# Scores of a streaming encoder's attention as 64-row matmuls on the two halves of TensorE

## The chip, the cores and the metric

One core of a Trainium2 chip runs the kernel. The metric is the device time of one execution in microseconds (us), the median of the runs.

## The reference, cut to what matters

One layer of a hybrid encoder, for a prompt of 2048 frames and a sample of 32 frames that continues a running stream (256 past frames). Everything is float32.

```python
h = rmsnorm(x, norm_gain)
qa, ka, va, ga, qb, kb, vb, gb = split(h @ w_in)          # 8 x 512 columns
# A: 8 heads x 64; each 64-frame chunk reads itself and 8 chunks before, with a relative bias
scores_a = einsum('bcqhd,bckhd->bchqk', qc, kband) * 64 ** -0.5 + bias
oa = softmax(scores_a) @ vband
# B: 4 heads, each with two 64-wide q/k pairs (m) and one 128-wide value, causal over chunks
scores_b = einsum('bqhmd,bkhmd->bhmqk', rope(qb), rope(kb)) * 64 ** -0.5
p = softmax(where(mask, scores_b, -inf))
ob = subnorm((p[:, :, 0] - lam * p[:, :, 1]) @ vb)
y = rmsnorm(x + concat(oa * silu(ga), ob * silu(gb)) @ w_out, final_gain)
```

The outputs are y and the new k and v rows, for prompt and sample.

## The kernel before

The work goes in eight units `u` of 128 columns: four of A (two heads of 64 each) and four of B (one head with two q/k pairs of 64 each). In both cases a unit has two score problems with a contraction over 64, called `m` = 0 and 1 here and "heads" below. Each unit walks over 8 chunks of 256 frames (two tiles `tt` of 128). For one chunk, `chunk_qkv` projects q, k, v and the gate on TensorE (PE), transposes q and k, and puts them where the score matmuls read them. `attn_a` or `attn_b` then computes scores, softmax and the product with v. The output projection follows after all units, and the 32 frames of the sample are worked in between.

Full float32 precision is made of float32r matmuls: a value is split into a high part and a low part (value minus high), and a product is the sum of several passes. The projections (L254 to L256, L261 to L263) take three passes: high x high, high x low, low x high.

The scores take two passes before, with 128 rows for a contraction over 64. `ks[:, m]` holds, for head m, the high part of k in one half of the 128 rows and the low part in the other half. `qh[:, m]` holds the high part of q in both halves, `ql[:, m]` the low part in the half that meets k's high part, and zero in the other (L132, L133). So pass 1 (L378) gives q-high x (k-high + k-low), pass 2 (L379) q-low x k-high. The stacking takes two casts on ScalarE (L335, L336), four scaled copies on ScalarE (L339 to L342) and four VectorE subtractions (L337, L338, L343, L344) per chunk and unit; there are 64 such steps.

The score matmuls write a PSUM buffer of 512 columns (`s_psum`, three buffers, L102). In `attn_b`, for each block of up to 512 keys and each m: the two passes, a maximum on VectorE (L466), an exponential on ScalarE (L468). In `attn_a`, for each m and tt: the band of up to 640 keys in one or two pieces, with VectorE adding the bias and taking the maximum (L526).

The order of the work on each engine is not that of the text. A scheduler sets it when the kernel is built, from a simulated timeline, from priorities (`ahead(n)` shifts them) and from free buffers; PE then executes its list strictly as written. A list is shown here with one row for each matmul, `out<-in`, with the number of the buffer behind its name: `s_ps` are score buffers, `z_ps` projections, `o_ps` products with v, `t_ps` transposes.

Of the kernel before, what the change touches and what calls it, by code (L numbers as in the profile page):

```python
# [8 lines left out]
F32 = mybir.dt.float32  # L9
F32R = mybir.dt.float32r  # L10
AF = mybir.ActivationFunctionType
ALU = mybir.AluOpType
# [18 lines left out]
def hybrid_step(  # L31
# [54 lines left out]
    @contextmanager  # L86
    def ahead(n):
        tc.cur_priority -= n
        yield
        tc.cur_priority += n  # L90
# [7 lines left out]
    def st_tile(name, n, bufs=4):  # L98
        return pool.tile([P, n], F32, name=name, tag=name, bufs=bufs)

    def s_psum():
        return psum.tile([P, 512], F32, name="s_ps", tag="s", bufs=3)  # L102
# [23 lines left out]
    nlam = const.tile([P, 1], F32, name="nlam")  # L126
    hTs = const.tile([P, KT, 2 * NS], F32R, name="hTs")
    oTs = const.tile([P, KT, 2 * NS], F32R, name="oTs")
    qh = [const.tile([P, 2, 256], F32R, name=f"qh{i}") for i in range(2)]
    ql = [const.tile([P, 2, 256], F32R, name=f"ql{i}") for i in range(2)]  # L130
    for t in ql:
        POOL.memset(t[64:128, 0, :].bitcast(F32), 0.0)  # L132
        POOL.memset(t[0:64, 1, :].bitcast(F32), 0.0)  # L133
    qzs = const.tile([P, 2, NS], F32, name="qzs")
    POOL.memset(qzs, 0.0)

# [160 lines left out]
    def chunk_qkv(u, isB, c, hT, W, kss, vts):  # L297
        z = pool.tile([P, 2, 384], F32, name="z", tag="z", bufs=2)
        z0 = 0 if isB else 128
        for tt in range(2):  # L300
            zp = z_psum()
            project(hT, tt, W, zp[:, z0:384], slice(z0, 384))
            ACT.copy(out=z[:, tt, z0:384], in_=zp[:, z0:384])
        if not isB:
            qp = z_psum()
            project_T(hT, W, qp[:, 0:256], slice(0, 128))
        i = u % 4
        if isB:
            zr = z[:, :, 0:256].rearrange("p t (g e) -> p t g e", g=4)
            rope(zr, ropec[:, 2 * c:2 * c + 2, :], ropes[:, 2 * c:2 * c + 2, :], P, 2)  # L310
        for tt in range(2):
            t = 2 * c + tt
            if isB:
                SP.dma_start(out=bkpv[t * P:(t + 1) * P, i * P:(i + 1) * P], in_=z[:, tt, 128:256])
                SP.dma_start(out=bvpv[t * P:(t + 1) * P, i * P:(i + 1) * P], in_=z[:, tt, 256:384])
            elif t >= 12:
                r0 = (t - 12) * P
                SP.dma_start(out=akpv[r0:r0 + P, i * P:(i + 1) * P], in_=z[:, tt, 128:256])
                SP.dma_start(out=avpv[r0:r0 + P, i * P:(i + 1) * P], in_=z[:, tt, 256:384])
        with ahead(150):  # L320
            tp = t_psum()
            for tt in range(2):
                PE.transpose(out=tp[:, tt * P:(tt + 1) * P], in_=z[:, tt, 128:256], identity=ident)
                if isB:
                    PE.transpose(out=tp[:, 256 + tt * P:256 + (tt + 1) * P], in_=z[:, tt, 0:128], identity=ident)
            if c % 2 == 0:
                kss.append(pool.tile([P, 2, 512], F32R, name="ks", tag="ks", bufs=5))
            ks = kss[c // 2][:, :, (c % 2) * 256:(c % 2 + 1) * 256]
            tk = tp[:, 0:256]
            tq = tp[:, 256:512] if isB else qp[:, 0:256]  # L330
            par = parity[0]
            parity[0] ^= 1
            QH, QL = qh[par], ql[par]
            lo_, hi_ = slice(0, 64), slice(64, 128)
            ACT.copy(out=ks[lo_, 0, :], in_=tk[lo_])  # L335
            ACT.copy(out=ks[hi_, 1, :], in_=tk[hi_])  # L336
            DVE.tensor_tensor(ks[hi_, 0, :], tk[lo_], ks[lo_, 0, :].bitcast(F32), ALU.subtract)  # L337
            DVE.tensor_tensor(ks[lo_, 1, :], tk[hi_], ks[hi_, 1, :].bitcast(F32), ALU.subtract)  # L338
            ACT.activation(QH[lo_, 0, :], tq[lo_], AF.Copy, scale=0.125)  # L339
            ACT.activation(QH[hi_, 0, :], tq[lo_], AF.Copy, scale=0.125)  # L340
            ACT.activation(QH[lo_, 1, :], tq[hi_], AF.Copy, scale=0.125)
            ACT.activation(QH[hi_, 1, :], tq[hi_], AF.Copy, scale=0.125)  # L342
            DVE.scalar_tensor_tensor(QL[lo_, 0, :], tq[lo_], 0.125, QH[lo_, 0, :].bitcast(F32), ALU.mult, ALU.subtract)  # L343
            DVE.scalar_tensor_tensor(QL[hi_, 1, :], tq[hi_], 0.125, QH[hi_, 1, :].bitcast(F32), ALU.mult, ALU.subtract)  # L344
        yield QH, QL
        with ahead(-30):
            gp = z_psum()
            project_T(hT, W, gp[:, 0:256], slice(384, 512))
        if c % 2 == 0:
            vtt = pool.tile([P, 4, 2, P], F32R, name="vt", tag="vt", bufs=5)  # L350
            vts.append(vtt[:, 0:2])
            vts.append(vtt[:, 2:4])
        vt = vts[c]
        zv = z[:, :, 256:384]
        if isB:
            vh, vl = vt[:, :, 0, :], vt[:, :, 1, :]
            POOL.tensor_scalar(vh, zv, 1.0, 0.0, ALU.mult, ALU.add)
            POOL.tensor_tensor(vl, zv, vh.bitcast(F32), ALU.subtract)
        else:
            for m in range(2):  # L360
                src = zv[:, :, 64 * m:64 * m + 64]
                vh = vt[:, :, m, 64 * m:64 * m + 64]
                vl = vt[:, :, m, 64 - 64 * m:128 - 64 * m]
                POOL.tensor_scalar(vh, src, 1.0, 0.0, ALU.mult, ALU.add)
                DVE.tensor_tensor(vl, src, vh.bitcast(F32), ALU.subtract)
        gate = silu(gp[:, 0:256], P, 256)
        yield gate

    def qk(sp, QH, QL, ks, m, tt, k0, k1):
        if k1 - k0 == 1:  # L370
            if k0 % 2:
                k0 -= 1
            else:
                k1 += 1
        qs = slice(tt * P, (tt + 1) * P)
        w = (k1 - k0) * P
        kc = slice(k0 * P, k1 * P)
        PE.matmul(sp[:, 0:w], QH[:, m, qs], ks[:, m, kc], start=True, stop=False)  # L378
        PE.matmul(sp[:, 0:w], QL[:, m, qs], ks[:, m, kc], start=False, stop=True)  # L379
        return k0  # L380

    def split_p(blocks, kind):
# [64 lines left out]
    def attn_b(u, c, kss, vts, QH, QL):  # L447
# [3 lines left out]
        for tt in range(2):  # L451
# [6 lines left out]
            for b in range(nb):  # L458
                w = min(512, nk - b * 512)
                eb = []  # L460
                for m in range(2):
                    sp = s_psum()
                    qk(sp, QH, QL, kss[b], m, tt, 0, w // P)
                    if b == nb - 1:
                        DVE.memset(sp[0:64, w - 64:w], NEG)
                    DVE.tensor_reduce(nmx[:, m, b:b + 1], sp[:, 0:w], AX.X, ALU.max, negate=True)  # L466
                    e = e_tile("e")
                    ACT.activation(e[:, 0:w], sp[:, 0:w], AF.Exp, bias=nmx[:, m, b:b + 1], accum_out=sm[:, m, b:b + 1])  # L468
                    eb.append(e)
                es.append((eb, w))  # L470
# [35 lines left out]
    def attn_a(u, c, kss, vts, QH, QL, bias):  # L506
        c0 = max(0, c - 2)
        kss, vts = list(kss), list(vts)
        rows = {}
        for m in range(2):  # L510
            for tt in range(2):
                t = 2 * c + tt
                k0 = max(0, t - 4)
                w = (t - k0 + 1) * P
                with ahead(-250):
                    nmx = st_tile("nma", 1, 6)
                    e = pool.tile([P, BAND], F32, name="ea", tag="ea", bufs=4)
                    ev = e[:, 0:w]
                    mx = None
                    for j in range(k0 // 4, t // 4 + 1):  # L520
                        ka, kb = max(k0, 4 * j), min(t + 1, 4 * j + 4)
                        sp = s_psum()
                        kf = qk(sp, QH, QL, kss[j], m, tt, ka - 4 * j, kb - 4 * j)
                        wd, es, bs, ss = (kb - ka) * P, (ka - k0) * P, (ka - t + 4) * P, (ka - 4 * j - kf) * P
                        m2 = st_tile("mxa", 1, 8)
                        DVE.tensor_tensor_reduce(e[:, es:es + wd], sp[:, ss:ss + wd], bias[:, m, bs:bs + wd], 1.0,  # L526
                                                 NEG if mx is None else mx, ALU.add, ALU.max, m2)
                        mx = m2
                    DVE.tensor_scalar(nmx, mx, -1.0, 0.0, ALU.mult, ALU.add)  # L529
                    sm = st_tile("sma", 1, 6)  # L530
                    ACT.activation(ev, ev, AF.Exp, bias=nmx, accum_out=sm)  # L531
                    DVE.reciprocal(sm, sm)  # L532
                    POOL.tensor_scalar(ev, ev, sm[:, 0:1], 0.0, ALU.mult, ALU.add)  # L533
                rows[m, tt] = (e, k0)
        gate, vtc = yield
        vts = vts[:c] + [vtc]
        op = o_psum()
# [289 lines left out]
```

## Time and profile before

| what | before |
|---|---|
| median of 3 runs | 1624.31 us (1621.44 to 1624.65) |
| the profiled execution's time (its span) | 1624.3 us |
| PE busy | 1568.4 us, 97% |
| PE weight loads busy | 1453.1 us, 89% |
| VectorE (DVE) busy | 1110.5 us, 68% |
| ScalarE (ACT) busy | 997.0 us, 61% |
| GpSimd (POOL) busy | 654.6 us, 40% |

Busy time is the time in which an engine had an instruction under way. PE's matmuls overlap in its pipeline, so a matmul's own duration is longer than its share of the time; the distance from one start to the next is what it costs.

### The profile page before, as it was taken

How to read it: one execution, taken by the hardware profiler on the slowest of the kernel's cores; microseconds unless marked ns; L12 is line 12 of the kernel's file. 1: busy time of each engine (PE TensorE's matmuls, PEld its weight loads, DVE VectorE, ACT ScalarE, POOL GpSimd, SP SyncE). 2: the span in 40 equal slices, each digit the busy share in tenths (PEclk: the TensorE clock that was granted, in tenths of full speed). 3: DMA queues.
4: the chain of work that ended last, by engine and by line, in shares of the span. 5: the costliest groups of instructions: out<-in, count | busy, mean ns of one | idle time of the engine just before them, and what ended most of it. 6: DMA issues, size and time to landing. Idle time of an engine off the chain costs nothing.

```text
span 1624.3 us, 30799 instructions
## 1 busy us (share of the span) xinstructions
PE 1568.4 (97%) x10612; PEld 1453.1 (89%) x10612; DVE 1110.5 (68%) x3048; ACT 997.0 (61%) x2717; POOL 654.6 (40%) x1129
## 2 busy tenths in 40 slices
PE   7999999989999899999999999999999999989997
PEld 6899999978998799999998899999998999978885
DVE  5776757897588866675788856676789677743333
ACT  5776557777577766656777766565777666531111
POOL 5453434465145544353345544353446444520000
PEclk9999999999999999999999999999999999999999
DMA  7643453333332224335432153344423263334562
GB/s 275 225 172 119 176 208 131 131 122 130 125 137 86 97 102 178 122 128 195 162 136 79 66 186 124 131 148 167 159 89 129 84 240 131 131 132 161 172 210 67
DMA packets 92972, 233.92 MB, mean 144 GB/s; under 512 B 9776, under 2 KB 51888, under 8 KB 75376
## 3 DMA queue, kind: packets, MB, share of 16 engines
q1 hardware_dynamic: 92816, 231.96, 40.0%
q8 instruction: 84, 1.38, 0.3%
q14 instruction: 72, 0.59, 0.1%
HBM read 179.10 MB, written 53.74 MB: 143 GB/s over the span
## 4 chain that ended last, share of the span: by engine, by line
PE 77%; DVE 11%; ACT 5%; issue 3%; POOL 2%; DMA 1%; SPq 0%; DVEq 0%; POOLq 0%; ACTq 0%
PE z_ps L254 11%; PE z_ps L255 11%; PE z_ps L256 11%; PE t_ps L387 6%; PE z_ps L261 5%; PE z_ps L263 5%; PE z_ps L262 5%; PE s_ps L379 4%; PE s_ps L378 4%; DVE nmx L466 2%; PE o_ps L556 2%; PE o_ps L555 2%; DVE e L479 2%; DVE w L174 2%; PE o_ps L501 1%
## 5 line engine op out<-in xcount | busy, mean ns | idle before, releaser
L255 PE MATMUL z_ps<-w,hT 128*128 128x256 f32 (+2 forms) x1280 | 424.1, 332 | 4.1 <-POOL w L171 2.4
L254 PE MATMUL z_ps<-w,hT 128*128 128x256 f32 (+2 forms) x1280 | 424.7, 332 | 2.5 <-ACT hT L229 1.2
L256 PE MATMUL z_ps<-w,hT 128*128 128x256 f32 (+2 forms) x1280 | 424.1, 331 | 0.0
L255 PEld LDWEIGHTS z_ps<-w,hT 128*128 128x128 f32 x1280 | 243.5, 190 | 22.4 <-POOL w L171 3.4
L254 PEld LDWEIGHTS z_ps<-w,hT 128*128 128x128 f32 x1280 | 243.7, 190 | 19.3 <-ACT hT L229 1.7
L468 ACT ACTIVATE e<-s_ps,nmx 128x512 f32<-128x512 f32 (+3 forms) x320 | 199.1, 624 | 98.6 <-DVE nmx L466 90.5
L256 PEld LDWEIGHTS z_ps<-w,hT 128*128 128x128 f32 x1280 | 243.7, 190 | 14.1 <-issue 0.5
L397 DVE TENSOR_TENSOR pl<-t_ps,ph 128x512 fp32r<-128x512 f32 (+1 forms) x312 | 192.6, 623 | 77.8 <-ACT ph L396 75.4
L261 PE MATMUL z_ps<-hT,w 128*128 128x256 f32 x768 | 220.3, 287 | 1.7 <-DVE ql L344 1.7
L263 PE MATMUL z_ps<-hT,w 128*128 128x256 f32 x768 | 218.9, 285 | 0.0
L396 ACT CAST ph<-t_ps 128x512 fp32r<-128x512 f32 (+1 forms) x312 | 163.0, 535 | 90.5 <-PE o_ps L555 42.4
L262 PE MATMUL z_ps<-hT,w 128*128 128x256 f32 x768 | 218.4, 284 | 0.0
L378 PE MATMUL s_ps<-ks,qh 128*128 128x512 f32 (+2 forms) x544 | 194.0, 366 | 10.5 <-ACT e L468 7.8
L466 DVE TENSOR_REDUCE nmx<-s_ps 128x1 f32<-128x512 f32 (+3 forms) x320 | 187.9, 600 | 13.1 <-PE s_ps L379 9.8
L379 PE MATMUL s_ps<-ks,ql 128*128 128x512 f32 (+2 forms) x544 | 187.7, 357 | 0.1
L474 POOL TENSOR_SCALAR e<-e,da 128x512 f32<-128x512 f32 (+3 forms) x160 | 110.3, 704 | 168.5 <-DVE da L444 132.8
L261 PEld LDWEIGHTS z_ps<-hT,w 128*128 128x128 f32 x768 | 145.5, 190 | 4.9 <-PE o_ps L416 1.2
L262 PEld LDWEIGHTS z_ps<-hT,w 128*128 128x128 f32 x768 | 145.4, 189 | 2.1 <-issue 0.5
L263 PEld LDWEIGHTS z_ps<-hT,w 128*128 128x128 f32 x768 | 145.4, 189 | 1.6 <-issue 0.5
L533 POOL TENSOR_SCALAR ea<-ea,sma 128x640 f32<-128x640 f32 (+4 forms) x128 | 96.3, 754 | 115.3 <-DVE sma L532 98.7
L531 ACT ACTIVATE ea<-ea,nma 128x640 f32<-128x640 f32 (+4 forms) x128 | 97.3, 760 | 62.6 <-DVE nma L529 61.4
L378 PEld LDWEIGHTS s_ps<-ks,qh 128*128 128x128 f32 x544 | 102.2, 190 | 19.3 <-ACT e L468 12.0
(192 smaller groups left out, 3422.3 us busy)
## 6 DMA issues: line engine op xcount, KB each, us to landing
hT<-hTd SPq DMA_DIRECT2D x112, 1024.0 KB, 7.0
wraw<-in_w_in_dram SPq DMA_DIRECT2D x64, 256.0 KB, 5.0
hTd<-hT SPq DMA_DIRECT2D x8, 2048.0 KB, 7.3
oTd<-oT SPq DMA_DIRECT2D x64, 256.0 KB, 3.2
hT<-oTd SPq DMA_DIRECT2D x16, 1024.0 KB, 6.1
out_dram<-z SPq DMA_DIRECT2D x160, 64.0 KB, 1.6
xt<-in_x_prompt_dram SPq DMA_DIRECT2D x32, 256.0 KB, 5.4
y<-in_x_prompt_dram SPq DMA_DIRECT2D x32, 256.0 KB, 6.5
```

The lines of the kernel that those rows point to most:

```text
L254: PE.matmul(zp, hT[:, 0, k, ts], his[k][:, cols], start=(k == 0), stop=False)
L255: PE.matmul(zp, hT[:, 0, k, ts], los[k][:, cols], start=False, stop=False)
L256: PE.matmul(zp, hT[:, 1, k, ts], his[k][:, cols], start=False, stop=(k == KT - 1))
L261: PE.matmul(zp, his[k][:, cols], hT[:, 0, k, :], start=(k == 0), stop=False)
L262: PE.matmul(zp, his[k][:, cols], hT[:, 1, k, :], start=False, stop=False)
L263: PE.matmul(zp, los[k][:, cols], hT[:, 0, k, :], start=False, stop=(k == KT - 1))
L378: PE.matmul(sp[:, 0:w], QH[:, m, qs], ks[:, m, kc], start=True, stop=False)
L379: PE.matmul(sp[:, 0:w], QL[:, m, qs], ks[:, m, kc], start=False, stop=True)
L396: ACT.copy(out=hv, in_=tv)
L397: DVE.tensor_tensor(lv, tv, hv.bitcast(F32), ALU.subtract)
L466: DVE.tensor_reduce(nmx[:, m, b:b + 1], sp[:, 0:w], AX.X, ALU.max, negate=True)
L468: ACT.activation(e[:, 0:w], sp[:, 0:w], AF.Exp, bias=nmx[:, m, b:b + 1], accum_out=sm[:, m, b:b + 1])
```

## The change

The stacking goes. q and k stay as the transposes leave them: head 0 in rows 0 to 63, head 1 in rows 64 to 127. `ks[:, 0]` is the high part of both heads' k, `ks[:, 1]` the low part; `qh` and `ql` likewise lose the index m. That takes one ScalarE and one VectorE operation over 128 rows each for k, and the same for q. A score is now made by three matmuls of 64 rows: q-high x k-high, q-high x k-low, q-low x k-high. `qk` takes two score buffers and writes, for each of the three terms, first head 0's matmul and then head 1's. `attn_b` and `attn_a` ask for both buffers ahead of `qk`, and treat the two heads behind it; `attn_a`'s loop over m moves inside that over tt.

```diff
-            lo_, hi_ = slice(0, 64), slice(64, 128)
-            ACT.copy(out=ks[lo_, 0, :], in_=tk[lo_])
-            ACT.copy(out=ks[hi_, 1, :], in_=tk[hi_])
-            DVE.tensor_tensor(ks[hi_, 0, :], tk[lo_], ks[lo_, 0, :].bitcast(F32), ALU.subtract)
-            DVE.tensor_tensor(ks[lo_, 1, :], tk[hi_], ks[hi_, 1, :].bitcast(F32), ALU.subtract)
-            ACT.activation(QH[lo_, 0, :], tq[lo_], AF.Copy, scale=0.125)
...
-            DVE.scalar_tensor_tensor(QL[hi_, 1, :], tq[hi_], 0.125, QH[hi_, 1, :].bitcast(F32), ALU.mult, ALU.subtract)
+            ACT.copy(out=ks[:, 0, :], in_=tk)
+            DVE.tensor_tensor(ks[:, 1, :], tk, ks[:, 0, :].bitcast(F32), ALU.subtract)
+            ACT.activation(QH, tq, AF.Copy, scale=0.125)
+            DVE.scalar_tensor_tensor(QL, tq, 0.125, QH.bitcast(F32), ALU.mult, ALU.subtract)
...
-        PE.matmul(sp[:, 0:w], QH[:, m, qs], ks[:, m, kc], start=True, stop=False)
-        PE.matmul(sp[:, 0:w], QL[:, m, qs], ks[:, m, kc], start=False, stop=True)
+        terms = ((QH, 0), (QH, 1), (QL, 0))
+        for n, (q, part) in enumerate(terms):
+            for m in range(2):
+                hs = slice(64 * m, 64 * m + 64)
+                PE.matmul(sps[m][:, 0:w], q[hs, qs], ks[hs, part, kc], start=(n == 0), stop=(n == 2))
...
-                for m in range(2):
-                    sp = s_psum()
-                    qk(sp, QH, QL, kss[b], m, tt, 0, w // P)
+                sps = [s_psum() for _ in range(2)]
+                qk(sps, QH, QL, kss[b], tt, 0, w // P)
+                for m, sp in enumerate(sps):
...
+                for j in range(k0 // 4, t // 4 + 1):
+                    ka, kb = max(k0, 4 * j), min(t + 1, 4 * j + 4)
+                    sps = [s_psum() for _ in range(2)]
+                    kf = qk(sps, QH, QL, kss[j], tt, ka - 4 * j, kb - 4 * j)
```

PE's list moves with it. The first place is where `attn_b` begins on a chunk in the second unit of B; the score buffers are 7007 (head 0), 7013 (head 1) and 7019 (head 0 of the next block) before, and L416 closes the chunk ahead. Before:

```order
L416 MATMUL o_ps_6848<-sq_6910,onesd_72 128x256
L378 MATMUL s_ps_7007<-ks_5604,qh1_85 128x512
L378 MATMUL s_ps_7013<-ks_5604,qh1_85 128x512
L378 MATMUL s_ps_7019<-ks_6150,qh1_85 128x512
L379 MATMUL s_ps_7007<-ks_5604,ql1_87 128x512
L379 MATMUL s_ps_7019<-ks_6150,ql1_87 128x512
L379 MATMUL s_ps_7013<-ks_5604,ql1_87 128x512
```

The same place in PE's list of the changed kernel; the score line is L372 there, 7043 and 7044 are the two heads of the first block, and 7057 is head 0 of the next.

```order
L372 MATMUL s_ps_7043<-ks_5640,qh1_85 128x512
L372 MATMUL s_ps_7044<-ks_5640,qh1_85 128x512
L409 MATMUL o_ps_6890<-sq_6952,onesd_72 128x256
L372 MATMUL s_ps_7043<-ks_5640,qh1_85 128x512
L372 MATMUL s_ps_7044<-ks_5640,qh1_85 128x512
L372 MATMUL s_ps_7043<-ks_5640,ql1_87 128x512
L372 MATMUL s_ps_7044<-ks_5640,ql1_87 128x512
L372 MATMUL s_ps_7057<-ks_6182,qh1_85 128x512 x2
L372 MATMUL s_ps_7057<-ks_6182,ql1_87 128x512
```

Here the two heads of the first block alternate, but for a 128-row matmul between them; the third buffer goes to head 0 of the next block, whose head 1 (7058) stands further down.

The second place is on PE some 80 rows later in the same chunk, where all three buffers are in use. Before, each head's two passes stand between other work:

```order
L378 MATMUL s_ps_7067<-ks_5604,qh1_85 128x512
L379 MATMUL s_ps_7067<-ks_5604,ql1_87 128x512
L254 MATMUL z_ps_7691<-w_5198,hT_7331 128x384
L255 MATMUL z_ps_7691<-w_5198,hT_7331 128x384
L256 MATMUL z_ps_7691<-w_5198,hT_7331 128x384
```

In the changed kernel, 7123 and 7124 are the two heads of one block there:

```order
L372 MATMUL s_ps_7123<-ks_6182,qh1_85 128x512 x2
L372 MATMUL s_ps_7123<-ks_6182,ql1_87 128x512
L380 MATMUL t_ps_7272<-ident_67,e_6765 128x128
L380 MATMUL t_ps_7272<-ident_67,e_6831 128x128 x2
L495 MATMUL o_ps_7209<-pl_7241,vt_6315 128x256
L493 MATMUL o_ps_7209<-ph_7240,vt_6315 128x256
L494 MATMUL o_ps_7209<-ph_7240,vt_6315 128x256
L372 MATMUL s_ps_7124<-ks_6182,qh1_85 128x512 x2
L372 MATMUL s_ps_7124<-ks_6182,ql1_87 128x512
```

The three passes of head 0 stand together, six 128-row matmuls follow, and then come the three passes of head 1.

## Rows read from the trace of the kernel before

**Rows 1.** The page's head: span, and busy time of each engine (share, instructions).
```profile
span 1624.3 us, 30799 instructions
...
PE 1568.4 (97%) x10612; PEld 1453.1 (89%) x10612; DVE 1110.5 (68%) x3048; ACT 997.0 (61%) x2717; POOL 654.6 (40%) x1129
```

**Rows 2.** Busy us by stretch: length, engines (instructions), clock, DMA share, GB/s.
```profile
600.00:800.00 200.00, 199.29 (x1470) 190.61 (x1469) 133.25 (x419) 126.03 (x339) 81.96 (x171) 1.00 0.41 148
```

**Rows 3.** Waits of PE: waiter, releaser, us in total, times, longest.
```profile
PE t_ps L226 <- POOL xt L209: 11.6, 2, 9.9
PE s_ps L378 <- ACT e L468: 7.8, 12, 1.2
...
PE s_ps L378 <- ACT qh L340: 1.6, 2, 1.4
```

**Rows 4.** Timeline of PE, six score matmuls: start us, modelled us, instruction.
```profile
995.32 0.39 PE L378 MATMUL s_ps<-ks,qh 128*128 128x512 f32 x1
995.55 0.39 PE L379 MATMUL s_ps<-ks,ql 128*128 128x512 f32 x1
995.78 0.28 PE L378 MATMUL s_ps<-ks,qh 128*128 128x256 f32 x1
995.90 0.28 PE L379 MATMUL s_ps<-ks,ql 128*128 128x256 f32 x1
996.02 0.34 PE L378 MATMUL s_ps<-ks,qh 128*128 128x384 f32 x1
996.19 0.34 PE L379 MATMUL s_ps<-ks,ql 128*128 128x384 f32 x1
996.37 0.28 PE L262 MATMUL z_ps<-hT,w 128*128 128x256 f32 x1
```

**Rows 5.** Groups by shape, the score's first pass: count | busy, mean ns | idle before.
```profile
L378 PE MATMUL s_ps<-ks,qh 128*128 128x512 f32 x280 | 114.1, 411 | 6.6 <-ACT e L468 4.8 <-ACT qh L340 1.6 <-ACT qh L342 0.2
...
L378 PE MATMUL s_ps<-ks,qh 128*128 128x256 f32 x176 | 51.0, 297 | 3.4 <-ACT e L468 3.0 <-ACT qh L342 0.4
...
L378 PE MATMUL s_ps<-ks,qh 128*128 128x384 f32 x88 | 31.4, 360 | 0.5 <-DVE mxa L526 0.5
```

**Rows 6.** Timeline of PE where 32-row transposes (32*128) stand among 128-row work.
```profile
604.84 0.38 PE L592 MATMUL t_ps<-ident,kvs 128*128 128x128 f32 x2
605.15 0.24 PE L593 MATMUL t_ps<-ident,zs 32*128 32x32 f32 x1
605.24 0.22 PE L594 MATMUL t_ps<-ident,zs 32*128 32x32 f32 x1
605.30 0.22 PE L595 MATMUL t_ps<-ident,gate 32*128 32x32 f32 x1
605.45 0.39 PE L502 MATMUL o_ps<-pl,vt 128*128 128x256 f32 x1
605.68 0.28 PE L500 MATMUL o_ps<-ph,vt 128*128 128x256 f32 x1
605.80 0.28 PE L501 MATMUL o_ps<-ph,vt 128*128 128x256 f32 x1
```

**Rows 7.** Timeline of PE at a second such place.
```profile
765.81 0.27 PE L325 MATMUL t_ps<-ident,z 128*128 128x128 f32 x1
766.01 0.43 PE L633 MATMUL t_ps<-ident,es 32*128 32x32 f32 x5
766.37 0.39 PE L261 MATMUL z_ps<-hT,w 128*128 128x256 f32 x1
766.60 0.28 PE L262 MATMUL z_ps<-hT,w 128*128 128x256 f32 x1
```

**Rows 8.** Groups by shape on ScalarE: count | busy, mean ns | idle before.
```profile
L287 ACT ACTIVATE gabs<-gate 128x256 f32<-128x256 f32 x64 | 26.7, 417 | 15.6 <-DVE gate L286 14.8
...
L335 ACT CAST ks<-t_ps 64x256 fp32r<-64x256 f32 x64 | 23.1, 361 | 20.6 <-PE t_ps L325 11.8 <-PE t_ps L323 8.1
...
L339 ACT ACTIVATE qh<-t_ps 64x256 fp32r<-64x256 f32 x32 | 12.0, 376 | 14.2 <-DVE ks L338 13.8
```

More of the change, by code (lines that the diff above doesn't have):

```diff
@@ L128, in hybrid_step @@
     oTs = const.tile([P, KT, 2 * NS], F32R, name="oTs")
[L129 to L133, printed above, removed]
+    qh = [const.tile([P, 256], F32R, name=f"qh{i}") for i in range(2)]
+    ql = [const.tile([P, 256], F32R, name=f"ql{i}") for i in range(2)]
     qzs = const.tile([P, 2, NS], F32, name="qzs")
@@ L333, in chunk_qkv @@
             QH, QL = qh[par], ql[par]
-            lo_, hi_ = slice(0, 64), slice(64, 128)
-            ACT.copy(out=ks[lo_, 0, :], in_=tk[lo_])
-            ACT.copy(out=ks[hi_, 1, :], in_=tk[hi_])
-            DVE.tensor_tensor(ks[hi_, 0, :], tk[lo_], ks[lo_, 0, :].bitcast(F32), ALU.subtract)
-            DVE.tensor_tensor(ks[lo_, 1, :], tk[hi_], ks[hi_, 1, :].bitcast(F32), ALU.subtract)
-            ACT.activation(QH[lo_, 0, :], tq[lo_], AF.Copy, scale=0.125)
[L340 to L343, printed above, removed]
-            DVE.scalar_tensor_tensor(QL[hi_, 1, :], tq[hi_], 0.125, QH[hi_, 1, :].bitcast(F32), ALU.mult, ALU.subtract)
+            ACT.copy(out=ks[:, 0, :], in_=tk)
+            DVE.tensor_tensor(ks[:, 1, :], tk, ks[:, 0, :].bitcast(F32), ALU.subtract)
+            ACT.activation(QH, tq, AF.Copy, scale=0.125)
+            DVE.scalar_tensor_tensor(QL, tq, 0.125, QH.bitcast(F32), ALU.mult, ALU.subtract)
         yield QH, QL
@@ L367, in chunk_qkv, with qk @@
         yield gate
-    def qk(sp, QH, QL, ks, m, tt, k0, k1):
+    def qk(sps, QH, QL, ks, tt, k0, k1):
         if k1 - k0 == 1:
@@ L509, in attn_a @@
         rows = {}
[L510 to L515, printed above, removed]
-                    nmx = st_tile("nma", 1, 6)
[L517 to L529, printed above, removed]
+        for tt in range(2):
+            t = 2 * c + tt
+            k0 = max(0, t - 4)
+            w = (t - k0 + 1) * P
+            with ahead(-250):
+                es_ = [pool.tile([P, BAND], F32, name="ea", tag="ea", bufs=4) for _ in range(2)]
+                mxs = [None, None]
+                for j in range(k0 // 4, t // 4 + 1):
+                    ka, kb = max(k0, 4 * j), min(t + 1, 4 * j + 4)
+                    sps = [s_psum() for _ in range(2)]
+                    kf = qk(sps, QH, QL, kss[j], tt, ka - 4 * j, kb - 4 * j)
+                    wd, es, bs, ss = (kb - ka) * P, (ka - k0) * P, (ka - t + 4) * P, (ka - 4 * j - kf) * P
+                    for m in range(2):
+                        m2 = st_tile("mxa", 1, 8)
+                        DVE.tensor_tensor_reduce(es_[m][:, es:es + wd], sps[m][:, ss:ss + wd], bias[:, m, bs:bs + wd], 1.0,
+                                                 NEG if mxs[m] is None else mxs[m], ALU.add, ALU.max, m2)
+                        mxs[m] = m2
+                for m in range(2):
+                    ev = es_[m][:, 0:w]
+                    nmx = st_tile("nma", 1, 6)
+                    DVE.tensor_scalar(nmx, mxs[m], -1.0, 0.0, ALU.mult, ALU.add)
@@ L533, in attn_a @@
                     POOL.tensor_scalar(ev, ev, sm[:, 0:1], 0.0, ALU.mult, ALU.add)
-                rows[m, tt] = (e, k0)
+                    rows[m, tt] = (es_[m], k0)
         gate, vtc = yield
```

## The prediction

> **What bounds the kernel now.** I read the busy totals first: TensorE (PE) is busy 1568.4 of 1624.3 us, so at most 55.9 us of the span are not matmul [rows 1]. The table by stretches shows that this is no average over unlike stages: in a stretch of 200 us in the middle PE is busy 199.3 us, with VectorE at 133 and ScalarE at 126 [rows 2]. The list of PE's waits says the same from the other side: the longest is the start, 11.6 us for the first normalised x; the waits of the score matmuls for a free score buffer come to 7.8 us, and those for the stacked q to 1.6 us [rows 3]. So the time is the sum of what PE's instructions take one after another, in the order in which the scheduler has written them. A change is priced by what it does to that sum; what it saves on ScalarE and VectorE counts only where PE waited for it.
>
> What a matmul costs is the distance between starts, since the durations shown are those of a pipeline. The timeline of PE has six score matmuls in a row [rows 4]: 995.32 to 995.55 to 995.78 is 0.23 us for 512 columns, 995.78 to 995.90 to 996.02 is 0.12 for 256, 996.02 to 996.19 to 996.37 is 0.175 for 384. Cost goes by columns alone, about 0.45 ns each.
>
> **The change part by part.**
>
> *Three passes instead of two.* There are 280 first passes of 512 columns, 176 of 256 and 88 of 384 [rows 5], and as many second passes. Now: 560 x 0.23 + 352 x 0.12 + 176 x 0.175 = 128.8 + 42.2 + 30.8 = 201.8 us. With three passes 840 x 0.23 + 528 x 0.12 + 264 x 0.175 = 302.7 us. A matmul of 64 rows streams as many columns as one of 128, so without any overlap the change costs +100.9 us.
>
> *Overlap of the two halves.* If the halves of the array work side by side, a matmul that stands directly behind one of the other head is free. How often it does is in PE's order, which is fixed before the run, and the kernel's own text (head 0, head 1, head 0, ...) is not what the scheduler made of it. Of the 1632 score matmuls only few keep an other-head neighbour, as the second of the two places shown with the change tells: with three score buffers, only one is usually free, so one head's three passes go out alone, other work follows, and the other head's three come later. Counted along the whole order, 353 neighbours are of different heads and 807 of the same; paired off, 94 matmuls of 512, 36 of 384 and 84 of 256 columns can be hidden: 94 x 0.23 + 36 x 0.175 + 84 x 0.12 = 38.0 us. No row here shows two halves at once (the 32-row matmuls of this trace all use the same rows), so the bounds are 0 and 38.0. I take 38.0, since different halves share neither weights nor a score buffer.
>
> The Trainium skill, page "TensorE: Matmul & The Clock Gate", section "Part 3: Packing small matmuls — row/col tiling", says that matmuls on distinct row groups start about 4 ns apart and that matmuls never overtake one another. By it the 38.0 us are gained, and not more, since a head's partner that stands behind other work cannot be pulled forward; by the rows alone it could be anything from 0.
>
> *Changing the height of the array.* Before, the prompt's matmuls are nearly all 128 rows high. Now the score matmuls stand in 472 runs among 128-row matmuls (308 of them three long), and every run is entered and left. What that costs is shown by the sample's few 32-row transposes [rows 6]. From the second 128-row transpose (two begin at 604.84 and take 0.11 each, so it starts at 604.95) it is 0.20 us to the first 32-row one, 0.09 over its 0.11. The first 32-row step is 0.09 where the next is 0.06: +0.03. The step out is 0.15: +0.09. The first 128-row matmul behind takes 605.45 to 605.68 = 0.23 where the next take 0.12: +0.11. In all 0.32 us. A second place [rows 7]: from 765.81 to 766.60 is 0.79 us for one transpose (0.11), five 32-row ones (5 x 0.06) and one matmul of 256 columns (0.12), 0.53 together: 0.26 us. That a 64-row run pays the same is not shown. From below it could be nothing, from above 0.32; the nearest rows say 0.26 to 0.32, and I take 0.30: 472 x 0.30 = 141.6 us.
>
> *Weight loads.* Each added matmul brings a load. In rows 4 the loads don't show in the distance between starts. In 32-row mode a transposition with its load has a step of 0.06 us (605.24 to 605.30) [rows 6], of which 32 columns at 0.45 ns are 0.014; so between 0 and 0.046 us of a load can stand open. I take 0, the reading of rows 4, and keep 1632 x 0.046 = 75 us for the range.
>
> *Stacking.* Two 64-row casts of k at 0.36 us and four 64-row scalings of q at 0.38 [rows 8] become one of each over 128 rows, at about 0.42 by the 128x256 activation [rows 8]; four VectorE operations become two. Over 64 steps that is 64 x (2.24 - 0.84) = 90 us of ScalarE, hidden under PE's work almost entirely: PE waited 1.6 us for it [rows 3]. The four memsets of ql at the start run beside the 11.6 us wait for x. With PE later by a tenth and the other engines lighter, some of the 55.9 us of idle PE time goes; the start stays, so at most 44 us. On the other hand both buffers of a pair are now filled before the second is emptied, which could double the 7.8 us wait for buffers. Between -44 and +8 I take -10.
>
> *Sum.* The profiled execution's span, 1624.3 us, is the median of the runs shown, 1624.31. 1624.3 + 100.9 - 38.0 + 141.6 - 10 = 1818.8; I say 1820.
>
> **The rivals.**
>
> No overlap of the halves: everything else as above, without the 38.0: 1857 us. For it: nothing in the trace shows two matmuls at once. Against: separate rows, buffers and weights.
>
> Open weight loads: in half-height mode the load of a head's next pass waits for the pass in front, as 807 neighbours of the same head invite. 1857 plus up to 75, 1857 to 1932 us. Against: the loads are covered in rows 4, and the 32-row steps of 0.06 us leave little. The Trainium skill, same page and section, says that a weight load overlaps a running matmul only where the row groups differ; rows 4 disagree at full height, and no row has half height.
>
> Cheap change of height: 128 to 64 rows costs little although 128 to 32 doesn't. With 0 to 0.15 us a run it is 1624.3 + 100.9 - 38.0 - 10 = 1677 to 1748 us: still slower, because of the order.
>
> Half-height matmuls at half price: PE keeps the two halves as separate queues, so that each 64-row matmul costs half, wherever its partner stands. The scores then take 151 us, 50 less than now. This alone gives 1574 us and is faster than before from the point where a run's two changes cost less than 50 / 472 = 0.11 us; at 0.30 it would be 1574 + 142 = 1716. Against it: matmuls start in the order written in every stretch that I read, and rows 6 and 7 show 0.26 to 0.32. With a price close to 0.11 it would end as no change.
>
> **How the numbers follow.** Forecast with the pairs overlapping and switches at 0.26 to 0.32: 40%, with its own range 1795 to 1840. No overlap: 20%. Open loads: 15%. Cheap change of height: 18%. Half price: 7%, of which 4 end faster, 1 the same, 2 slower still. For 8 in 10 I leave out the top of the open loads and the lower half of the cheap changes: 1700 to 1890 us. A measurement of this kernel tells about 0.2% (3 us) from no change; beyond that faster 4%, the same 1%, slower 95%.
>
> **What the profile after would show.** PE's matmul count grows by 544 and its busy share stays near 97%. The score line has 1632 matmuls of 64 rows. Runs of one head step by 0.23 us at 512 columns; a pair of different heads starts almost together, then steps by 0.23. Into and out of a run of three PE's timeline shows about 0.1 us of extra distance at each of several places, 0.3 in all, and over an undisturbed stretch the same projection work takes longer by that. ScalarE's busy time falls by about 90 us. PE's waits for other engines don't grow. Wrong would be: starts at the edges of a run no farther apart than inside (then 1680 to 1720); distances of 0.28 us or more between the passes of one head at 512 columns (then towards 1900); or a new long wait of PE for a score buffer, which the sum has at 8 us at most.

## The result and the profile after

The changed kernel takes 1816.75 us (median of 4 runs, 1815.9 to 1819.11), the kernel before 1624.32; the ratio is 1.1187, with a 95% interval of 1.1171 to 1.1203. It is slower by 192 us.

The page of the changed kernel, its head and the score line (the columns are those of [rows 1] and [rows 5]):

```profile
span 1814.1 us, 31318 instructions
...
PE 1779.2 (98%) x11156; PEld 1490.7 (82%) x11156; DVE 1055.9 (58%) x2920; ACT 911.5 (50%) x2461; POOL 659.0 (36%) x1125
...
L372 PE MATMUL s_ps<-ks,qh 64*128 64x512 f32 (+2 forms) x1088 | 297.3, 398 | 0.6 <-ACT e L461 0.6
...
L372 PE MATMUL s_ps<-ks,ql 64*128 64x512 f32 (+2 forms) x544 | 169.0, 354 | 0.0
```

Against [rows 1], PE has 544 matmuls more and is idle for 34.9 us instead of 55.9; ScalarE is 85 us less busy, VectorE 55. Most of that relief lies beside a PE that has become longer; what of it PE got back is told further down.

PE's waits after, answering to [rows 3]:

```profile
PE t_ps L223 <- POOL xt L206: 11.0, 2, 10.8
...
PE s_ps L372 <- ACT e L461: 0.6, 1, 0.6
```

The waits of the score matmuls for a buffer fell from 7.8 us to 0.6, and the one for the stacked q is gone. The time is in PE's own list. Its timeline at the second place that was shown with the change, with the first of the two score runs:

```profile
564.54 0.28 PE L494 MATMUL o_ps<-ph,vt 128*128 128x256 f32 x1
564.66 0.39 PE L266 MATMUL z_ps<-w,hTs 128*64 128x512 f32 x1
564.98 0.72 PE L372 MATMUL s_ps<-ks,qh 64*128 64x512 f32 x2
565.55 0.39 PE L372 MATMUL s_ps<-ks,ql 64*128 64x512 f32 x1
565.87 0.55 PE L380 MATMUL t_ps<-ident,e 128*128 128x128 f32 x3
```

At [rows 4] a matmul of 512 columns had 0.23 us to the next start. Here L266 has 0.32 (564.66 to 564.98), the two passes with q-high together 0.57 instead of 0.46, and the last pass 0.32 instead of 0.23. So 0.09 us are lost going into the run, about 0.10 on its second matmul and 0.09 going out. The weight loads (PEld) of the same place:

```profile
564.55 0.14 PEld L266 LDWEIGHTS z_ps<-w,hTs 128*64 128x64 f32 x1
564.98 0.29 PEld L372 LDWEIGHTS s_ps<-ks,qh 64*128 64x128 f32 x2 [0.30 <-issue]
565.32 0.18 PEld L372 LDWEIGHTS s_ps<-ks,ql 64*128 64x128 f32 x1
```

The load of the run's third matmul starts at 565.32, a whole step ahead of that matmul at 565.55. The load of its first matmul does not start ahead: it starts at 564.98 together with the matmul. Over the trace, a load in full-height work starts 0.003 us behind the start of the matmul in front of its own; at a change of height the first load starts with its own matmul (0.002 us ahead), and the second one starts 0.107 us behind that matmul's start (medians). The second matmul is late by nearly the same 0.10 us. That the late loads are what delays the matmuls is a reading of these rows; no run tests it.

The next place shows the fourth piece, and what a pair does: both heads side by side, six 64-row matmuls in a row.

```profile
980.39 0.28 PE L493 MATMUL o_ps<-ph,vt 128*128 128x256 f32 x1
980.51 0.28 PE L494 MATMUL o_ps<-ph,vt 128*128 128x256 f32 x1
980.72 0.74 PE L372 MATMUL s_ps<-ks,qh 64*128 64x512 f32 x4
981.29 0.40 PE L372 MATMUL s_ps<-ks,ql 64*128 64x512 f32 x2
981.62 0.39 PE L495 MATMUL o_ps<-pl,vt 128*128 128x256 f32 x1
981.84 0.28 PE L493 MATMUL o_ps<-ph,vt 128*128 128x256 f32 x1
981.96 0.28 PE L494 MATMUL o_ps<-ph,vt 128*128 128x256 f32 x1
```

Six matmuls of 512 columns take 980.72 to 981.62 = 0.90 us, not 6 x 0.23 = 1.38: the halves do overlap. But 980.51 to 980.72 is 0.21 where 256 columns take 0.12, and behind the run 981.62 to 981.84 is 0.22 before the step is 0.12 again. A run thus pays 0.09 + 0.10 + 0.09 + 0.10. Over the whole trace the medians of these four, each the distance to the next start less the usual one for the same columns, are 0.092, 0.104, 0.088 and 0.104 us, 0.39 together.

### The profile page after: what moved, and what is told of

Its sections match the earlier page's. It is cut to its first block, busy times and chain, and to the rows that moved or that the text cites. A ratio compares the mean times of both kernels' runs of the same rounds, so it can differ in the third digit from the quotient of the medians.

```text
span 1814.1 us, 31318 instructions
## 1 busy us (share of the span) xinstructions
PE 1779.2 (98%) x11156; PEld 1490.7 (82%) x11156; DVE 1055.9 (58%) x2920; ACT 911.5 (50%) x2461; POOL 659.0 (36%) x1125
## 4 chain that ended last, share of the span: by engine, by line
PE 93%; DVE 2%; DMA 2%; issue 1%; ACT 1%; POOL 0%; SPq 0%; DVEq 0%; POOLq 0%; ACTq 0%
PE s_ps L372 18%; PE z_ps L251 12%; PE z_ps L252 12%; PE z_ps L253 11%; PE t_ps L380 7%; PE z_ps L258 5%; PE z_ps L259 5%; PE z_ps L260 5%; PE o_ps L549 2%; PE o_ps L550 2%; PE o_ps L493 2%; PE o_ps L495 2%; PE o_ps L494 2%; PE z_ps L265 1%; PE z_ps L266 1%
## 5 line engine op out<-in xcount | busy, mean ns | idle before, releaser
L372 PE MATMUL s_ps<-ks,qh 64*128 64x512 f32 (+2 forms) x1088 | 297.3, 398 | 0.6 <-ACT e L461 0.6
L258 PE MATMUL z_ps<-hT,w 128*128 128x256 f32 x768 | 224.6, 292 | 0.0
L259 PE MATMUL z_ps<-hT,w 128*128 128x256 f32 x768 | 222.1, 289 | 0.0
L260 PE MATMUL z_ps<-hT,w 128*128 128x256 f32 x768 | 221.6, 289 | 0.0
L372 PEld LDWEIGHTS s_ps<-ks,qh 64*128 64x128 f32 x1088 | 141.4, 185 | 78.9 <-issue 29.0
L372 PE MATMUL s_ps<-ks,ql 64*128 64x512 f32 (+2 forms) x544 | 169.0, 354 | 0.0
```

The source lines that it names most:

```text
L258: PE.matmul(zp, his[k][:, cols], hT[:, 0, k, :], start=(k == 0), stop=False)
L259: PE.matmul(zp, his[k][:, cols], hT[:, 1, k, :], start=False, stop=False)
L260: PE.matmul(zp, los[k][:, cols], hT[:, 0, k, :], start=False, stop=(k == KT - 1))
L372: PE.matmul(sps[m][:, 0:w], q[hs, qs], ks[hs, part, kc], start=(n == 0), stop=(n == 2))
```

## The experiments

**e1: the change of height alone.** The half of `ql` that the kernel before multiplies by zero can be left out without changing the result, so its second pass can have 64 rows while everything else stays.

```diff
-        PE.matmul(sp[:, 0:w], QL[:, m, qs], ks[:, m, kc], start=False, stop=True)
+        hs = slice(64 * m, 64 * m + 64)
+        PE.matmul(sp[:, 0:w], QL[hs, m, qs], ks[hs, m, kc], start=False, stop=True)
```

> The kernel before, with its second pass alone (q-low x k-high) on 64 rows; the half left out of it is zero anyway, so columns, passes and stacking stay as they are. PE's order has 514 runs of 64-row matmuls, 492 of them a single one. Theory A (from the changed kernel's trace: 0.09 us into a run, 0.10 on the second matmul in it, 0.09 out of it, 0.10 on the second matmul behind it): a run of one pays 0.09 + 0.09 + 0.10 = 0.28 us, 514 x 0.28 = 146 us, less up to 35 us of waits for score buffers that go when PE is later: 1735 to 1770 us. Theory B (changing the height is cheap; the changed kernel is slow by its third pass and by slow 64-row matmuls): 1625 to 1660 us.

Measured: 1775.32 us, ratio 1.0927 (1.0902 to 1.0952), +150 us for work that is otherwise the same: in the traces, 10610 of PE's 10612 matmuls stand at the same place in the order as before. Theory B falls; theory A is low by 5 to 40 us. A run of one in this kernel's timeline:

```profile
586.54 0.28 PE L502 MATMUL o_ps<-ph,vt 128*128 128x256 f32 x1
586.66 0.40 PE L378 MATMUL s_ps<-ks,qh 128*128 128x512 f32 x1
586.99 0.49 PE L380 MATMUL s_ps<-ks,ql 64*128 64x512 f32 x1
587.41 0.39 PE L254 MATMUL z_ps<-w,hT 128*128 128x256 f32 x1
587.63 0.28 PE L255 MATMUL z_ps<-w,hT 128*128 128x256 f32 x1
587.75 0.28 PE L256 MATMUL z_ps<-w,hT 128*128 128x256 f32 x1
```

L378 has 0.33 us (+0.10), the one 64-row matmul 0.42 (+0.19), L254 0.22 (+0.10). A run of one pays the same 0.39 us as a run of three: I had left out 0.10 because there is no second matmul in it, but it falls on the way out. 514 x 0.39 = 200 us of edges, of which 150 arrive: PE's idle time falls from 55.9 to 1776.3 - 1742.1 = 34.2 us, and its granted clock rises from 0.987 to 0.991 of full, worth about 5 us. That is some 27 of the missing 50 us; the rest stands in no list of waits.

**e2: the third pass alone.** The second pass is made twice, on 128 rows.

```diff
-        PE.matmul(sp[:, 0:w], QL[:, m, qs], ks[:, m, kc], start=False, stop=True)
+        PE.matmul(sp[:, 0:w], QL[:, m, qs], ks[:, m, kc], start=False, stop=False)
+        PE.matmul(sp[:, 0:w], QL[:, m, qs], ks[:, m, kc], start=False, stop=True)
```

> The kernel before with a third 128-row pass: the second pass is made twice (its term is counted double in the scores). No change of height, stacking kept. Theory A: only 201.8 x 0.5 = 100.9 us of columns are added, less 20 to 50 us of waits and half-rate clock that go when PE is denser: 1675 to 1705 us. Theory B (the whole loss is passes): 1780 us or more, as in the changed kernel.

Measured: 1686.33 us, ratio 1.0385 (1.0369 to 1.04). Of 100.9 us of columns 62 arrive; that is inside the range of theory A, and theory B falls.

```profile
span 1684.4 us, 31881 instructions
...
PE 1648.3 (98%) x11156; PEld 1530.4 (91%) x11156; DVE 1115.9 (66%) x3048; ACT 1004.4 (60%) x2717; POOL 661.9 (39%) x1129
```

It has the 11156 matmuls of the changed kernel and all the stacking of the kernel before, and is 130 us faster than the changed kernel. PE is idle for 36.1 us against 55.9, and its granted clock is 0.996 against 0.987, which is worth 1624.3 x 0.013 - 1684.4 x 0.004 = about 14 us. These two are 34 of the 39 us that don't arrive. PE's other matmuls are in a new order here too, so that a part can be the order's.

**e3: no overlap.** In the changed kernel both heads use rows 0 to 63. PE's order is the same row by row.

```diff
-                hs = slice(64 * m, 64 * m + 64)
+                hs = slice(0, 64)
```

> The changed kernel with both heads' score matmuls in rows 0 to 63 (head 1 gets head 0's scores). PE's order is the same row by row; only the other half of the array is never used, so nothing can overlap. Theory A (neighbours of different heads overlap wholly): the 38 us of the prediction come back, up to 45 with what the second pairs hide: 1850 to 1865 us. Rival (halves don't overlap): 1817 us, no difference.

Measured: 1861.87 us, 45 us above the changed kernel (ratios to the kernel before 1.1462, 1.1445 to 1.1479, against 1.1187). That is inside the range of theory A, and the rival falls. The place of the six matmuls from above:

```profile
1005.70 0.28 PE L494 MATMUL o_ps<-ph,vt 128*128 128x256 f32 x1
1005.91 0.73 PE L372 MATMUL s_ps<-ks,qh 64*128 64x512 f32 x2
1006.48 0.39 PE L372 MATMUL s_ps<-ks,ql 64*128 64x512 f32 x1
1006.71 0.63 PE L372 MATMUL s_ps<-ks,qh 64*128 64x512 f32 x2
1007.19 0.39 PE L372 MATMUL s_ps<-ks,ql 64*128 64x512 f32 x1
1007.50 0.38 PE L495 MATMUL o_ps<-pl,vt 128*128 128x256 f32 x1
1007.73 0.28 PE L493 MATMUL o_ps<-ph,vt 128*128 128x256 f32 x1
```

1005.91 to 1007.50 is 1.59 us against 0.90, which is three matmuls of 0.23 more; edges and everything else are equal. Overlap is real and complete where the order allows it. Inside the run 1006.48 to 1006.71 is 0.23: later weight loads of the same half don't stand open, only those at each change of height.

**e4: the stacking alone.** The kernel before with one cast, one scaled copy and two subtractions over 128 rows per step.

```diff
+            ACT.copy(out=ks[:, 0, :], in_=tk)
+            DVE.tensor_tensor(ks[:, 1, :], tk, ks[:, 0, :].bitcast(F32), ALU.subtract)
+            ACT.activation(QH[:, 0, :], tq, AF.Copy, scale=0.125)
+            DVE.scalar_tensor_tensor(QL[:, 0, :], tq, 0.125, QH[:, 0, :].bitcast(F32), ALU.mult, ALU.subtract)
...
-        PE.matmul(sp[:, 0:w], QH[:, m, qs], ks[:, m, kc], start=True, stop=False)
-        PE.matmul(sp[:, 0:w], QL[:, m, qs], ks[:, m, kc], start=False, stop=True)
+        PE.matmul(sp[:, 0:w], QH[:, 0, qs], ks[:, m, kc], start=True, stop=False)
+        PE.matmul(sp[:, 0:w], QL[:, 0, qs], ks[:, m, kc], start=False, stop=True)
```

> The kernel before with the changed kernel's two ScalarE and two VectorE operations per step in place of the six and four; the score matmuls stay two passes of 128 rows (they then mix the heads' terms). Theory A: PE's work is unchanged and PE hardly waited for the stacking: 1605 to 1624 us, ScalarE about 90 us less busy. Rival (the stacking is on the path, and the change gives something back by it that the sum doesn't show): 1590 us or less.

Measured: 1602.02 us, ratio 0.9864 (0.9849 to 0.9879): 23 us faster, just below the range of theory A and above the rival's bound.

```profile
span 1600.0 us, 30307 instructions
...
PE 1555.3 (97%) x10612; PEld 1445.7 (90%) x10612; DVE 1041.7 (65%) x2920; ACT 900.0 (56%) x2461; POOL 664.2 (42%) x1129
```

The same 10612 matmuls: 11 us less idle and 13 less busy, the latter with a granted clock of 0.993 instead of 0.987. But PE's order is not the same: only 4860 of them stand at the same place in the list, since the scheduler made a new order for the shorter stacking. Without the stacking, and in that order, the kernel is 23 us faster, though the waits of the score matmuls that name it [rows 3] were 1.6 us. Whether the gain comes from ScalarE and VectorE being free for what PE waits for elsewhere, or from the new order, is not shown.

**e5 and e6: all pairs side by side.** In the changed kernel the two heads' score buffers become one tile of two banks, twice; the transposes give up one of their two buffers for it. e6 is the kernel before with four score buffers and one for the transposes.

```diff
+    def s_pair():
+        sp2 = psum.tile([P, 2, 512], F32, name="s_ps", tag="s", bufs=2)
+        return [sp2[:, 0, :], sp2[:, 1, :]]
...
-        return psum.tile([P, 512], F32, name="t_ps", tag="t", bufs=2)
+        return psum.tile([P, 512], F32, name="t_ps", tag="t", bufs=1)
```

> The changed kernel with the two heads' score buffers as one tile of two banks, two such tiles (one transpose buffer instead of two makes the room). In PE's order the heads now always alternate: 1632 matmuls in 272 runs instead of 472, and every one has its partner beside it. Theory A (a run costs 0.39 us on both edges together, an overlapped pair costs one of its matmuls): scores 151 us instead of 202, -51; 272 x 0.39 = +106; less waits, stacking and half-rate clock as in the changed kernel, 30 to 50: 1630 to 1650 us, and on top whatever the lost transpose buffer costs (e6). So 0 to 25 us above e6, and clearly below the changed kernel's 1817. Theory B (the prediction's 0.30 us a run): 25 us less. Rival (the slowness is in the 64-row matmuls themselves): 1750 us or more.

> Control for e5: the kernel before with four score buffers and one transpose buffer, nothing else. Theory A: PE waits more for transposes to be emptied, less for scores: 1630 to 1660 us. Rival (PE's order makes good for it): 1620 to 1628 us.

Measured: 1913.23 us (1.1775, 1.1752 to 1.1798) and 1910.17 us (1.1764, 1.1744 to 1.1784). Both expectations in absolute time fail by 250 us and more, and e5 is not below the changed kernel: a transpose buffer given up for a fourth score buffer costs the kernel before 286 us. Head of e6, and two of its waits of PE:

```profile
PE 1691.0 (89%) x10612; PEld 1498.5 (79%) x10612; DVE 1119.8 (59%) x3048; ACT 1003.7 (53%) x2717; POOL 648.9 (34%) x1129
```

```profile
PE z_ps L255 <- ACT z L304: 30.3, 37, 1.3
PE t_ps L388 <- DVE pl L398: 21.6, 47, 2.5
```

PE's waits now stand at projections, transposes and products alike. Its order is a new one too (2537 of 10612 matmuls at their old place), and no run separates the order from the missing buffer. PE's busy share falls from 97% to 89% and its granted clock from 0.987 to 0.964. The difference of e5 and e6, +3 us, lies where theory A put it (0 to 25), but with PE no longer the only bound it decides nothing. What e5's trace does show is that the pairing works as expected: there are 272 runs, 813 matmuls start within 0.02 us of the one in front, and a run's edges still cost 0.39 us (median of the 82 runs without a wait). Whether the changed kernel would break even with all pairs side by side stays open: no run tries it with both transpose buffers kept.

**e7 and e8: what e4 points to.** GpSimd makes two of the four copies of q from SBUF, everything else as before; in e8 it also casts the gated output.

```diff
             ACT.activation(QH[lo_, 0, :], tq[lo_], AF.Copy, scale=0.125)
-            ACT.activation(QH[hi_, 0, :], tq[lo_], AF.Copy, scale=0.125)
-            ACT.activation(QH[lo_, 1, :], tq[hi_], AF.Copy, scale=0.125)
             ACT.activation(QH[hi_, 1, :], tq[hi_], AF.Copy, scale=0.125)
+            POOL.tensor_scalar(QH[hi_, 0, :], QH[lo_, 0, :].bitcast(F32), 1.0, 0.0, ALU.mult, ALU.add)
+            POOL.tensor_scalar(QH[lo_, 1, :], QH[hi_, 1, :].bitcast(F32), 1.0, 0.0, ALU.mult, ALU.add)
```

> The kernel before, where GpSimd copies the high part of q into the other half of the rows (two copies per step) in place of two of ScalarE's four scaled copies; scores and order of passes as before. If the 23 us that went with the stacking were ScalarE's time, half of its four q copies should give 5 to 12 us: 1612 to 1620 us. If they were the length of the chain from the transposes to the first score, or VectorE's time, GpSimd's copies are no shorter: 1622 us or more.

> As e7, and the cast of the gated output (128x256, once per step, 26 us of ScalarE in all) goes from ScalarE to GpSimd too, where its neighbours in the chain already are. If ScalarE's time is what PE's last waits come from: another 3 to 6 us, 1605 to 1610 us. If GpSimd at 44% busy begins to be late itself: 1612 us or more.

Measured: e7 1612.61 us, ratio 0.9932 (0.9916 to 0.9948), the fastest version here with the kernel's full work; e8 1617.97 us, ratio 0.9943 (0.9929 to 0.9956). e7 lands in its range. e8 gains nothing more than e7, as its second expectation had it, though ScalarE is busy for 22 us less than in e7. PE's waits in e8 name none of the copies that GpSimd took over, so that GpSimd is late there is not shown. In both kernels the scheduler made a new order for PE (6430 of e7's 10612 matmuls stand at the same place as before), so neither separates ScalarE's time from the order. Head of e7:

```profile
PE 1558.9 (97%) x10612; PEld 1447.0 (90%) x10612; DVE 1108.4 (69%) x3048; ACT 951.6 (59%) x2589; POOL 710.8 (44%) x1257
```

The group of one of the two copies in e7:

```profile
L341 POOL TENSOR_SCALAR qh<-qh 64x256 fp32r<-64x256 f32 x64 | 26.9, 420 | 87.2 <-ACT qh L339 77.5 <-ACT qh L340 3.4 <-DVE rr L190 2.9
```

With e7 ScalarE is 45 us less busy, GpSimd 56 more, and PE is idle for 51.4 us of a 1610.3 us span.

## Why the prediction was right, and where only its sum was

The time, 1816.75 us, is 3 us from the 1820 forecast and inside the likeliest case's own range. The mechanism held for the columns, the overlap and the edges of the runs; for the waits it did not. The sizes of three terms were off, and that their errors cancel to 3 us is luck. (The sum also started from a span and was set against a time; where both are on record the time is 1.8 us longer, 1815.9 against 1814.1 in the changed kernel.)

| term | predicted, us | measured | by |
|---|---|---|---|
| third pass, columns | +100.9 | +100.9 of columns (0.23 us each 512, as in [rows 4]) | trace after; e2 shows 62 of it net |
| overlap of the halves | -38.0 | -43 to -45 | trace after, e3 |
| edges of 472 runs | +141.6 (0.30 each) | +184 (0.39 each) | trace after, e1 |
| stacking and waits of PE | -10 | about -48 | what is left of 192; e4 shows 23 for the stacking with a new order |

*Order, not text.* That only some pairs stand together was read from PE's order ahead of the run, and the trace has the matmuls line by line in that order. The best that the change could reach, scores in half of 302.7 us (151) instead of 201.8, was never within reach in it.

*Overlap.* The bounds were 0 and 38.0, and the upper one was too low. In the trace 231 score matmuls (112 of 512 columns, 47 of 384, 72 of 256) start within 0.03 us of the one in front, which is 42.6 us at the prices of [rows 4]; my count had 214. e3 gives 45, with a granted clock of 0.992 against 0.994. The rival without overlap falls by the same run.

*Edges.* [Rows 6] and [rows 7] gave 0.32 and 0.26 us from 32-row transposes, where the second matmul in the run showed only +0.03. At 64 rows it shows +0.10; these matmuls differ from the transposes of [rows 6] in columns, in number format and in the weights they load, and no run separates the three. The term was short by 42 us. (That a matmul's cost goes by columns alone, 0.45 ns each, holds for the score matmuls of [rows 4] and not for these transposes: 0.11 us for 128 columns is 0.86 ns each.) The rival of a cheap change of height (1677 to 1748 us) is refuted by e1, where nothing else changed.

*Open weight loads.* The rival is wrong as put (every load of the same half): in e3, the third and later passes of a run step by 0.23. The loads at a change of height do start late, by the rows of PEld above, and the distance of 0.33 us on the second matmul, which the prediction had as a sign towards 1900 us, appears once per run; it is part of the 0.39.

*Half price.* Refuted: passes of the same half step by 0.23 us at 512 columns, like 128 rows.

*Waits.* This is the step that was furthest out. I bounded the term between -44 and +8 and took -10, near the 1.6 us of waits that name the stacked q; what is left of the 192 us is about -48, outside the bounds. Three readings led there. The stretch in [rows 2] is the densest of the four between 200 and 1000 us; in the other three PE was idle for 6 to 7 us of 200, at a lower clock:

```profile
200.00:400.00 200.00, 193.44 (x1224) 179.79 (x1223) 156.71 (x390) 138.59 (x386) 96.78 (x138) 0.97 0.43 152
400.00:600.00 200.00, 193.84 (x1302) 180.60 (x1302) 148.00 (x367) 139.76 (x384) 88.59 (x127) 0.98 0.32 112
800.00:1000.00 200.00, 193.23 (x1378) 181.26 (x1377) 153.30 (x400) 141.52 (x383) 94.53 (x147) 0.98 0.33 120
```

The list of waits names the stacking for more than 1.6 us: there are also 0.6 us for qh of L342, and 1.7 us of projections waiting for ql of L344, which in A reads q out of a projection buffer. And the score matmuls themselves were not at their price: summed from start to start, those of the kernel before take 231 us, not 201.8. Of the 29 us between, 11 stand as idle time, 3 are at half the clock, and 15 stand in no list of waits.

PE's idle time falls by 21 us in the changed kernel, its granted clock rises from 0.987 to 0.994, and by the share of the clock that alone is 1624.3 x 0.013 - 1814.1 x 0.006 = about 10 us. This part is uncertain: the clocks of other runs overlap, 0.985 to 0.993 for the kernel before and 0.990 to 0.994 for the changed one. With the 15 us of delays that no list names, which in the changed kernel can't be told from the edges of the runs, this makes up 46 of the 48.

e4 shows 23 us for the stacking and the new order alone, and e2, where the stacking is kept, loses only 62 of 100.9 us. The net figures of e1, e2, e3 and e4 can't be added: 150 x 472 / 514 + 62 - 45 - 23 = 132 us, not 192, because e1, e2 and e4 each give back some of the same 55.9 us of idle time (34.2, 36.1 and 44.7 are left) and of the same half-rate clock. Had this term been read as well as the others, the forecast with 0.30 us edges would have been 1624.3 + 100.9 - 38.0 + 141.6 - 48 = 1781 us.

## What to carry to other kernels

Price a matmul of fewer rows by where it stands: in this kernel each excursion from 128-row to 64-row matmuls and back cost 0.39 us, more than a whole matmul of 512 columns. By these numbers, an estimate, three paired passes save 0.23 us per block of 512 columns for two heads against four full ones, so a run must hold at least two such blocks to pay for its edges; no run here shows half-height work paying. Count the runs and the pairs in the order that the scheduler wrote, not in the source. And when PE is at 97%, a busier PE gives back part of what is added to it (here 39 of 101 us in e2), so the few per cent of idle time and of half-rate clock are a term of the sum with a size of its own.

## What the runs showed of the hardware that was not expected

A change between 128-row and 64-row matmuls delays two starts, not one: the first matmul in the new height by 0.09 us and the second by 0.10, in both directions (0.092, 0.104, 0.088, 0.104 us, medians in the changed kernel; the same 0.39 us in e1 with a single matmul between). With it the weight loads lose their lead: the first load behind the change starts with its own matmul, not with the one in front.

Two score matmuls on the two halves, which no row before showed, start mostly 3 to 10 ns apart and cost as much as one: 0.90 us for six against 1.59 on one half.

GpSimd copies 64 rows of 256 float32 from one half of SBUF's rows to the other in 0.42 us on average (e7); ScalarE's copy out of PSUM takes 0.38 [rows 8].

One transpose buffer instead of two cost 286 us of 1624 (e6), although a score buffer was gained: PE's waits spread over projections, products and transposes, none above 31 us in total. PE's order changed with it.
